# A decoder layer in split float32: other 16-byte places for the high weights of the up-projection and for the weights of the down-projection

## The chip, the cores and the metric

The kernel runs on one NeuronCore of a Trainium2 chip. The metric is device time in microseconds (us) of one execution. The kernel before takes 1066.99 us (median of 2 runs, 1066.96 to 1067.03).

## The reference

One layer for 256 tokens, model width 2048, all in float32. `w_in` feeds 16 heads of sliding-window attention with sinks and 16 heads of forgetting attention; the two groups are normalised, joined and go through `w_out`; then comes a gated MLP (5632 wide) with a causal convolution of width 3 between the up-projection and the activation. Every sub-layer is wrapped in two norms. What the change touches is the MLP:

```python
h = rmsnorm(x, pre_ffn_g[l])
u = causal_dwconv(h @ w_up[l], conv_w[l], conv_b[l])
gate, val = jnp.split(u, 2, axis=-1)
y = (jax.nn.gelu(gate, approximate=True) * val) @ w_down[l]
x = x + rmsnorm(y, post_ffn_g[l])
```

## The kernel before

**Split numbers.** [...] A product is then three matmuls: high by high, low by high, high by low. Weights come from HBM by SyncE's DMA queue into `raw` (512 KB, a ring of 5 buffers, line 71), ScalarE casts `raw` to the high part `whi` (line 117), VectorE subtracts to get the low part `wlo` (line 120). `whi` and `wlo` are rings of 5 buffers each. One such load is a *unit*.

**Up-projection: the weights are held.** `proj_T` (called 43 times for `w_up` with the order `LONG`, and with another order for `w_in`) makes 256 output columns. Its 16 k-tiles are four units of 4. In a matmul of a held weight, 128 columns of the weight are the stationary operand and `hT` (the activations, high and low side by side) is the moving operand: line 261 streams 512 columns of `hT` (high and low at once) past `whi`, line 268 streams 256 columns (high alone) past `wlo`. A unit gives 8 matmuls of each kind. `LONG = ((0, 1), (0, 1, 2, 3), (2, 3))` means: high of units 0 and 1, then low of units 0 to 3, then high of units 2 and 3. Since the next projection begins with its high units 0 and 1, TensorE sees runs of 32 high matmuls (512 columns) and runs of 32 low matmuls (256 columns) in turn. The first gate projection is written out by itself (lines 879 and 884), and its place in the program is not touched.

**Down-projection: the weights move.** For each half of the 5632 rows and each chunk of 512 output columns, 11 units of two k-tiles are loaded; `mm3` (line 283) holds 128 columns of the activations `G` and streams 512 columns of `whi`, `wlo`, `whi` past them: 12 matmuls a unit, 132 a chunk. Seven chunks go through the loop that the change touches (four of the first half, three of the second); the last chunk is written out apart.

**Places.** Buffers in SBUF lie on whole multiples of 256 bytes here. The kernel may start the data of a weight some 16-byte steps into its buffer. *Place* in this document means that number of steps (place 4 is 64 bytes in; place 16 is 256 bytes in). Before, all high parts and all moving weights are at place 0, as are `hT`, `G` and `oT`; the low parts of held weights are at `LOW = (14, 4, 4, 4)` for the units 0 to 3 of an up-projection, and at 14 and 4 in turn for `w_in` (function `w_parts`). The buffers of `whi` are 4096 bytes apart, those of `wlo` 4608.

**Order.** TensorE's instructions are kept in program order. The order on every other engine follows from the scheduler and, in some stretches, from manual order.

Of the kernel before, what the change touches and what calls it, by code (L numbers as in the profile page):

```python
# [8 lines left out]
F32 = mybir.dt.float32  # L9
F32R = mybir.dt.float32r  # L10
# [7 lines left out]
P = 128  # L18
# [7 lines left out]
FHALF = 22  # L26
HOLD = 6
LOW = (14, 4, 4, 4)
ROOM = 112


@with_exitstack
def hybrid_layer(ctx: ExitStack, tc: tile.TileContext, x, pre_mix_g, w_in, b_forget, sinks,
# [13 lines left out]

    small.tile([P, ROOM], F32, tag="room", bufs=1, name="room")
    ctx.enter_context(tc.manual_schedule(engines={mybir.EngineType.PE}))
# [7 lines left out]
    def tick():  # L57
        now[0] += 1
        for f in todo.pop(now[0], []):
            f()  # L60
# [5 lines left out]
    UNIT = 1024  # L66
    WB = 5

    def w_load(src, a, c, pin=False):
        raw = wp.tile([P, UNIT], F32, tag="raw", bufs=5, name="raw")  # L70
        i = sp.dma_start(raw[:, :a * c].rearrange("p (a c) -> p a c", a=a), src)
        if pin:
            tc.keep_in_program_order(i)
        return raw, a, c

    unit, period = [0], [2]

    def w_parts(n, keep=None, held=True):

        if keep and keep[0] is None:  # L80
            return keep[1]
        where, pre, nb = (keep[0], "h", keep[1]) if keep else (wp, "w", WB)
        hi = where.tile([P, UNIT], F32R, tag=pre + "hi", bufs=nb, name="whi")
        if where is not wp:
            lo = where.tile([P, UNIT], F32R, tag=pre + "lo", bufs=nb, name="wlo")
            return hi[:, :n], lo[:, :n]
        lo = where.tile([P, UNIT + 128], F32R, tag=pre + "lo", bufs=nb, name="wlo")
        at = 0
        if held:
            at = LOW[unit[0] % period[0]] * 4  # L90
            unit[0] += 1
        return hi[:, :n], lo[:, at:at + n]

    def w_high(unit, keep=None, held=True):

# [10 lines left out]
    def w_split(unit, pin=False, keep=None, begun=None, between=None,  # L106
                held=True):

        raw, a, c = unit
        n = a * c  # L110
        hi, lo = begun or w_parts(n, keep, held)
        for i in range(2 if between else 1):
            cs = slice(i * 512, i * 512 + 512) if between else slice(0, n)
            if i:
                between()
            if not between or i:
                i1 = act.copy(hi[:, cs], raw[:, cs])  # L117
                if pin:
                    tc.keep_in_program_order(i1)
            i2 = dve.tensor_tensor(lo[:, cs], raw[:, cs], hi[:, cs].bitcast(F32), op=ALU.subtract)  # L120
            if pin:
                tc.keep_in_program_order(i2)
        return [x.rearrange("p (a c) -> p a c", a=a) for x in (hi, lo)]

    def w_unit(src, a, c, keep=None):
        return w_split(w_load(src, a, c), keep=keep, held=False)

    def w_rows(w, k0, a, c0, c):
        return w[k0 * P:(k0 + a) * P, c0:c0 + c].rearrange("(a p) c -> p a c", p=P)
# [18 lines left out]
    for i in range(2):  # L148
        cs = slice(i * 256, (i + 1) * 256)
# [96 lines left out]
    def proj_T(w, c0, banks, runs=((0, 1), (0, 1), (2, 3), (2, 3))):  # L246

        parts, last = {}, ((len(runs) - 1) % 2, KT - 1)
        unit[0], period[0] = 0, 4 if len(runs) == 3 else 2

        def get(u):
            if u not in parts:
                parts[u] = w_split(w_load(w_rows(w, u * 4, 4, c0, 256), 4, 256))
            return parts[u]

        def high(u):
            hi = get(u)[0]
            for a in range(4):
                kt = u * 4 + a
                for m, b in enumerate(banks):  # L260
                    pe.matmul(b, hi[:, a, m * P:(m + 1) * P], hT[:, kt, 0:512], start=(kt == 0),  # L261
                              stop=(last == (0, kt)))

        def low(u):
            lo = get(u)[1]
            for a in range(4):
                for m, b in enumerate(banks):
                    pe.matmul(b[:, 256:512], lo[:, a, m * P:(m + 1) * P],  # L268
                              hT[:, u * 4 + a, 0:256], start=False,
                              stop=(last == (1, u * 4 + a)))  # L270

        for n, us in enumerate(runs):
            for u in us:
                (low if n % 2 else high)(u)
                tick()
# [13 lines left out]
    with tc.tile_pool(name="mixp", bufs=1) as mp:  # L289
# [311 lines left out]
        for p0, npair, cols in ((0, 3, 384), (3, 3, 384), (6, 2, 272)):  # L601
# [3 lines left out]
            for k0 in range(0, KT, per):  # L605
                na = min(per, KT - k0)
                hi, lo = w_unit(w_rows(w_in, k0, na, c0, cols), na, cols)
# [211 lines left out]
    with tc.tile_pool(name="ffn", bufs=1) as fp:  # L819
# [86 lines left out]
        for half in range(2):  # L906
            G = [fp.tile([P, 512], F32R, tag="G", bufs=FHALF, name=f"G{j}")[:, 0:512]
                 for j in range(FHALF)]
            for g in range(FHALF // 2):
                c0 = (half * (FHALF // 2) + g) * 256  # L910
                alt = g % 2
                if half == 0 and g == 0:
                    bg = first_gate()
                    order.__exit__(None, None, None)
                    bv = [bank(), bank()]
                    proj_T(w_up, DFF + c0, bv, LONG)
                else:
                    bg = [bank("att"), bank("att")] if alt else [bank(), bank()]
                    proj_T(w_up, c0, bg, LONG)
                gates = []  # L920
                for m in range(2):
                    y = conv(bg[m], c0 // P + m, "yg")
                    act.activation(y, y, AF.Gelu_apprx_tanh)
                    gates.append(y)
                if half or g:
                    bv = [bank("att"), bank("att")] if alt else [bank(), bank()]
                    proj_T(w_up, DFF + c0, bv, LONG)
                for m in range(2):
                    y = conv(bv[m], 44 + c0 // P + m, "yv")
                    dve.tensor_tensor(y, y, gates[m], op=ALU.mult)  # L930
                    gt = G[g * 2 + m]
                    split(gt[:, 0:256], gt[:, 256:512], y)
            if half == 1:
                rest = main.tile([P, KT, 512], F32R, tag="hT", name="rest")
                gbf = fp.tile([P, D], F32, tag="gbc", name="gbc_ffn")
                sp.dma_start(gbf, post_ffn_g[0].partition_broadcast(P))
                whole, halves = slice(0, 512), [slice(0, 256), slice(256, 512)]
                b1 = [bank("att"), bank("att")]
                for b, cs in zip(b1, halves):
                    pe.matmul(b[:, cs], G[0][:, 0:P], G[0][:, 0:256], start=True, stop=False)  # L940
                    act.copy(b[:, cs], y_sb[:, 1, 1536:2048][:, cs])

            def down(t, n, b):
                ys = y_sb[:, t, n * 512:(n + 1) * 512]
                if half == 0:
                    act.copy(ys, b)
                else:
                    dve.tensor_tensor(ys, b, ys, op=ALU.add)
                    act.activation(junk, ys, AF.Square, scale=D ** -0.5,
                                   accum_out=ysq[t][:, n:n + 1])  # L950
                    pool.tensor_tensor(ys, ys, gbf[:, n * 512:(n + 1) * 512], op=ALU.mult)

            LAST = FHALF // 2 - HOLD
            for n in range(3 + (half == 0)):
                b2 = [bank(), bank()]
                for u in range(FHALF // 2):
                    hi, lo = w_unit(w_rows(w_down, half * FHALF + u * 2, 2, n * 512, 512), 2, 512)
                    for a in range(2):
                        k = u * 2 + a
                        for t in range(2):  # L960
                            mm3(b2[t], G[k], t, hi[:, a, :], lo[:, a, :], slice(0, 512), k == 0,
                                k == FHALF - 1)
                for t in range(2):
                    down(t, n, b2[t])
# [32 lines left out]
        for u in range(FHALF // 2):  # L997
            hi, lo = w_unit(w_rows(w_down, FHALF + u * 2, 2, 1536, 512), 2, 512,
                            keep=(None, [rest[:, c:c + 2, :].rearrange("p a c -> p (a c)")
                                         for c in (4 * (u - LAST), 4 * (u - LAST) + 2)])  # L1000
                            if LAST <= u < FHALF // 2 - 4 else None)
# [13 lines left out]
        r = rstd_y(0, 3, v)  # L1015
        for n in range(4):
            finish(0, slice(n * 512, (n + 1) * 512), r, sp)
        last = fp.tile([P, 256], F32, tag="last", name="last")
        for h in range(2):
            if h:  # L1020
                v = before_last(1, 4)
# [38 lines left out]
```

## Time and profile before

| | |
|---|---|
| median of the runs | 1066.99 us |
| the profiled execution: its time, its span | 1067.17 us, 1065.3 us |
| TensorE matmul (PE) busy | 1055.4 us, 5974 instructions |
| weight loads (PEld) busy | 919.2 us, 5974 instructions |
| VectorE (DVE), ScalarE (ACT), GpSimd (POOL) busy | 738.3, 614.0, 226.2 us |
| mean granted TensorE clock | 0.998 |
| HBM read | 199.58 MB |

The span runs from the first to the last instruction; the 1.9 us between it and the execution's own time lie around it. Matmuls are pipelined, so the duration of one matmul (389 to 391 ns at 512 columns) is not what it costs. What it costs is the step from one matmul to the next, and that is read from the chain of waits: a piece there gives the start, the length and the number of matmuls, and the length divided by the number is the step. A row such as "7.29 PE bank_acc L261 x32" is a step of 228 ns.

### The profile page before, as it was taken

How to read it: one execution, taken by the hardware profiler on the slowest of the kernel's cores; microseconds unless marked ns; L12 is line 12 of the kernel's file. 1: busy time of each engine (PE TensorE's matmuls, PEld its weight loads, DVE VectorE, ACT ScalarE, POOL GpSimd, SP SyncE). 2: the span in 40 equal slices, each digit the busy share in tenths (PEclk: the TensorE clock that was granted, in tenths of full speed). 3: DMA queues.
4: the chain of work that ended last, by engine and by line, in shares of the span. 5: the costliest groups of instructions: out<-in, count | busy, mean ns of one | idle time of the engine just before them, and what ended most of it. 6: DMA issues, size and time to landing. Idle time of an engine off the chain costs nothing.

```text
span 1065.3 us, 16215 instructions
## 1 busy us (share of the span) xinstructions
PE 1055.4 (99%) x5974; PEld 919.2 (86%) x5974; DVE 738.3 (69%) x1200; ACT 614.0 (58%) x1062; POOL 226.2 (21%) x250
## 2 busy tenths in 40 slices
PE   9999999999999999999999999999999999999997
PEld 7889988888889888888888888888888888888886
DVE  5989868886568877777677444457777777755563
ACT  6776757767548655556565443456565555644450
POOL 4353245440122312112121000002121212201110
PEclk9999999999999999999999999999999999999999
DMA  8645667545863766566666666666666666666642
GB/s 290 191 127 175 181 191 213 176 153 160 296 223 122 236 197 193 183 198 197 197 187 185 202 196 195 194 186 198 183 199 192 195 181 198 197 195 194 192 170 79
DMA packets 164970, 202.88 MB, mean 190 GB/s; under 512 B 6780, under 2 KB 130972, under 8 KB 164380
## 3 DMA queue, kind: packets, MB, share of 16 engines
q1 hardware_dynamic: 164572, 201.45, 61.2%
q8 instruction: 47, 0.77, 0.3%
q10 hardware_dynamic: 320, 0.40, 0.1%
q14 instruction: 31, 0.25, 0.1%
HBM read 199.58 MB, written 2.11 MB: 189 GB/s over the span
## 4 chain that ended last, share of the span: by engine, by line
PE 94%; DVE 2%; issue 1%; DMA 1%; ACT 1%; POOL 1%; SPq 0%; DVEq 0%; POOLq 0%; ACTq 0%
PE bank_acc L283 34%; PE bank_acc L261 22%; PE bank_att L261 14%; PE bank_acc L268 11%; PE bank_att L268 7%; PE bank_att L449 1%; PE bank_att L484 1%; PE bank_att L493 1%; DVE wlo L120 1%; PE bank_acc L879 1%; PE bank_att L283 1%; DMA x_in<-in_x_dram 1%; PE bank_att L495 0%; PE bank_att L732 0%; POOL scr L416 0%
## 5 line engine op out<-in xcount | busy, mean ns | idle before, releaser
L120 DVE TENSOR_TENSOR wlo<-raw,whi 128x1024 fp32r<-128x1024 f32 (+3 forms) x357 | 435.7, 1230 | 239.1 <-ACT whi L117 232.7
L117 ACT CAST whi<-raw 128x1024 fp32r<-128x1024 f32 (+3 forms) x356 | 363.3, 1035 | 269.2 <-issue 121.2
L261 PE MATMUL bank_acc<-hT,whi 128*128 128x512 f32 x1088 | 260.6, 391 | 0.0
L261 PEld LDWEIGHTS bank_acc<-hT,whi 128*128 128x128 f32 x1088 | 200.1, 188 | 39.5
L283 PE MATMUL bank_acc<-whi,G 128*128 128x512 f32 x652 | 202.7, 389 | 0.0
L855 POOL TENSOR_TENSOR u<-u,rowf 128x256 f32<-128x256 f32 x88 | 96.6, 1118 | 493.5 <-DVE u L854 490.6
L261 PE MATMUL bank_att<-hT,whi 128*128 128x512 f32 x640 | 150.6, 390 | 0.0
L283 PEld LDWEIGHTS bank_acc<-whi,G 128*128 128x128 f32 x652 | 122.4, 188 | 25.0
L261 PEld LDWEIGHTS bank_att<-hT,whi 128*128 128x128 f32 x640 | 118.7, 188 | 23.9
L268 PEld LDWEIGHTS bank_acc<-hT,wlo 128*128 128x128 f32 x1088 | 131.1, 188 | 3.3
L268 PE MATMUL bank_acc<-hT,wlo 128*128 128x256 f32 x1088 | 133.4, 278 | 0.0
L283 PE MATMUL bank_acc<-wlo,G 128*128 128x512 f32 x326 | 126.9, 389 | 0.0
L283 PE MATMUL bank_acc<-whi,oT 128*128 128x512 f32 (+1 forms) x272 | 81.7, 379 | 0.0
L268 PEld LDWEIGHTS bank_att<-hT,wlo 128*128 128x128 f32 x640 | 76.0, 188 | 1.7
L268 PE MATMUL bank_att<-hT,wlo 128*128 128x256 f32 x640 | 76.3, 277 | 0.0
L283 PEld LDWEIGHTS bank_acc<-wlo,G 128*128 128x128 f32 x326 | 61.2, 188 | 12.3
L283 PEld LDWEIGHTS bank_acc<-whi,oT 128*128 128x128 f32 x272 | 50.2, 188 | 9.3
L283 PE MATMUL bank_acc<-wlo,oT 128*128 128x512 f32 (+1 forms) x136 | 51.2, 377 | 0.0
L283 PE MATMUL bank_acc<-whi,hT 128*128 128x384 f32 (+1 forms) x192 | 46.9, 323 | 0.0
L857 ACT ACTIVATE yg<-u,cw 128x256 f32<-128x256 f32 x44 | 26.5, 602 | 27.5 <-POOL u L855 27.5
L857 ACT ACTIVATE yv<-u,cw 128x256 f32<-128x256 f32 x44 | 26.4, 603 | 26.5 <-POOL u L855 26.5
L416 POOL TENSOR_TENSOR scr<-scr 128x256 f32<-128x256 f32 x26 | 26.7, 1042 | 57.2 <-DVE scr L415 34.3
(212 smaller groups left out, 1056.5 us busy)
## 6 DMA issues: line engine op xcount, KB each, us to landing
raw<-in_w_up_dram SPq DMA_DIRECT2D x176, 512.0 KB, 4.1
raw<-in_w_down_dram SPq DMA_DIRECT2D x88, 512.0 KB, 4.7
raw<-in_w_in_dram SPq DMA_DIRECT2D x51, 512.0 KB, 4.7
raw<-in_w_out_dram SPq DMA_DIRECT2D x32, 512.0 KB, 4.7
raw<-in_w_in_dram SPq DMA_DIRECT2D x16, 384.0 KB, 3.3
cb<-c_dram SPq DMA_DIRECT2D x8, 256.0 KB, 4.3
x_sb<-in_x_dram SPq DMA_DIRECT2D x2, 1024.0 KB, 5.9
raw<-in_w_in_dram SPq DMA_DIRECT2D x5, 408.0 KB, 4.1
```

Source lines behind the costliest of these rows:

```text
L117: i1 = act.copy(hi[:, cs], raw[:, cs])
L120: i2 = dve.tensor_tensor(lo[:, cs], raw[:, cs], hi[:, cs].bitcast(F32), op=ALU.subtract)
L261: pe.matmul(b, hi[:, a, m * P:(m + 1) * P], hT[:, kt, 0:512], start=(kt == 0), stop=(last == (0, kt)))
L268: pe.matmul(b[:, 256:512], lo[:, a, m * P:(m + 1) * P], hT[:, u * 4 + a, 0:256], start=False, stop=(last == (1, u * 4 + a)))
L283: pe.matmul(b, a, r[:, cols], start=(first and i == 0), stop=(last and i == 2))
L416: pool.tensor_tensor(dst, dst, row, op=ALU.mult)
L449: pe.matmul(sb[e][:, cs], a[r, t * P:(t + 1) * P], b[r, 0:nk], start=(n == 0), stop=(n == 2))
L484: pe.transpose(pb[:, i * P:(i + 1) * P], p[:, e, c:c + P], ident)
L493: pe.matmul(ov, values(hl, 0), p[:, :, 0:256], start=(n == 0), stop=False)
L855: pool.tensor_tensor(u[:, 2:258], u[:, 2:258], rowf, op=ALU.mult)
L857: act.activation(y, u[:, 2:258], AF.Identity, bias=cw[:, 3, ch:ch + 1], scale=cw[:, 2, ch:ch + 1])
L879: pe.matmul(v(b, t), gate[kt][0][:, ms], v(hT[:, kt, 0:512], t), start=(t == 0 and kt == 0), stop=False)
```

## The change

It changes where weights lie in their buffers, and nothing else: on each of the five engines the same instructions stand in the same order, with the same waits.

- The high parts of held weights in `w_up` get a place from the table `HIGH`. A row of it serves one run of 32 high matmuls: units 2 and 3 of a projection and units 0 and 1 of the next. There are 43 rows; of the last, only two entries are used. The first two units of all have place 0.
- The moving weights of `w_down` get places from the table `MOVE`: a row for each of the seven chunks, a pair (high part, low part) for each of the 11 units.
- The buffers of `whi` and `wlo` are all 4352 bytes apart now. The two rings take as many bytes together as before.
- The tile `last` of the final stretch takes a buffer of the ring `cs` in place of one of its own.
- The places of low parts of held weights stay as they were (`LOW`), and so do the high parts in `w_in` and `w_out`, and the last chunk of `w_down` (place 0).

```diff
 LOW = (14, 4, 4, 4)
+HIGH = (
+    (1,1,1,1), (2,2,2,2), (3,3,3,3), (4,4,4,4), (5,5,5,5), (6,6,6,6), (7,7,7,7),
+    (8,8,8,8), (9,9,9,9), (10,10,10,10), (11,11,11,11), (12,12,12,12), (13,13,13,13), (14,14,14,14),
+    (15,15,15,15), (2,4,4,4), (14,4,4,4), (12,4,4,4), (8,4,4,4), (10,4,4,4), (4,2,2,2),
+    (2,3,3,3), (0,4,4,4), (0,2,2,2), (0,1,1,1), (4,8,8,8), (8,12,12,12), (4,0,0,0),
+    (14,0,0,0), (2,0,0,0), (8,0,0,0), (12,0,0,0), (6,0,0,0), (0,2,4,6), (2,4,6,8),
+    (4,8,12,16), (1,2,3,4), (6,4,2,0), (0,4,0,4), (0,8,0,8), (0,16,0,16), (2,4,2,4),
+    (0,1,0,1),
+)
+MOVE = (
+    ((2, 2), (2, 2), (4, 4), (4, 4), (4, 4), (4, 4),
+     (12, 12), (12, 12), (4, 4), (4, 4), (4, 4)),
+    ((1, 1), (1, 1), (1, 1), (3, 3), (3, 3), (3, 3),
+     (5, 5), (5, 5), (5, 5), (6, 6), (6, 6)),
+    ((8, 8), (8, 8), (8, 8), (10, 10), (10, 10), (10, 10),
+     (14, 14), (14, 14), (14, 14), (16, 16), (16, 16)),
+    ((0, 4), (0, 4), (0, 4), (4, 0), (4, 0), (4, 0),
+     (0, 2), (0, 2), (0, 2), (0, 8), (0, 8)),
+    ((14, 14), (4, 4), (4, 4), (4, 4), (14, 14), (0, 0),
+     (0, 0), (0, 0), (2, 2), (0, 0), (0, 0)),
+    ((0, 0), (0, 0), (0, 0), (0, 0), (0, 0), (0, 0),
+     (12, 12), (12, 12), (12, 12), (15, 15), (15, 15)),
+    ((7, 7), (7, 7), (7, 7), (9, 9), (9, 9), (9, 9),
+     (11, 11), (11, 11), (11, 11), (13, 13), (13, 13)),
+)
...
-    unit, period = [0], [2]
+    unit, period, spot, turn_of = [0], [2], [(0, 0)], [-1]
...
-        hi = where.tile([P, UNIT], F32R, tag=pre + "hi", bufs=nb, name="whi")
         if where is not wp:
+            hi = where.tile([P, UNIT], F32R, tag=pre + "hi", bufs=nb, name="whi")
             lo = where.tile([P, UNIT], F32R, tag=pre + "lo", bufs=nb, name="wlo")
             return hi[:, :n], lo[:, :n]
-        lo = where.tile([P, UNIT + 128], F32R, tag=pre + "lo", bufs=nb, name="wlo")
-        at = 0
+        hi = where.tile([P, UNIT + 64], F32R, tag=pre + "hi", bufs=nb, name="whi")
+        lo = where.tile([P, UNIT + 64], F32R, tag=pre + "lo", bufs=nb, name="wlo")
+        (h, l), spot[0] = spot[0], (0, 0)
         if held:
-            at = LOW[unit[0] % period[0]] * 4
+            l = LOW[unit[0] % period[0]]
             unit[0] += 1
-        return hi[:, :n], lo[:, at:at + n]
+        return hi[:, h * 4:h * 4 + n], lo[:, l * 4:l * 4 + n]
...
         unit[0], period[0] = 0, 4 if len(runs) == 3 else 2
+        turn_of[0] += len(runs) == 3
 
         def get(u):
             if u not in parts:
+                j = turn_of[0] - (u < 2)
+                spot[0] = (HIGH[j][(u + 2) % 4] if j >= 0 else 0, 0)
                 parts[u] = w_split(w_load(w_rows(w, u * 4, 4, c0, 256), 4, 256))
             return parts[u]
...
                 for u in range(FHALF // 2):
+                    spot[0] = MOVE[half * 4 + n][u]
                     hi, lo = w_unit(w_rows(w_down, half * FHALF + u * 2, 2, n * 512, 512), 2, 512)
...
-        last = fp.tile([P, 256], F32, tag="last", name="last")
+        last = fp.tile([P, 256], F32, tag="cs", bufs=3, name="last")
```

## The prediction

> **What bounds the kernel now.** I read the page first, then TensorE's own waits, then the chain of waits stretch by stretch. The page:
>
> ```profile
> PE 1055.4 (99%) x5974; PEld 919.2 (86%) x5974; DVE 738.3 (69%) x1200; ACT 614.0 (58%) x1062; POOL 226.2 (21%) x250
> PEclk9999999999999999999999999999999999999999
> PE 94%; DVE 2%; issue 1%; DMA 1%; ACT 1%; POOL 1%; SPq 0%; DVEq 0%; POOLq 0%; ACTq 0%
> ```
>
> The waits of TensorE, all of them:
>
> ```profile
> PE bank_acc L172 <- DVE junk L167: 1.3, 1, 1.3
> PE bank_att L493 <- DVE pl L287: 0.4, 1, 0.4
> ```
>
> TensorE is busy 99% of the span at full granted clock, 94% of the chain is its own work, and it waits 1.7 us for others. So the time is the sum of its steps, and this change can act only on the step from one matmul to the next. The steps in the MLP, from the chain of waits (start, length, what; the steps are length by count):
>
> ```profile
> 386.47 7.29 PE bank_acc L261 x32
> 393.75 3.65 PE bank_acc L268 x32
> 576.10 119.68 PE bank_acc L283 x528
> 936.70 90.47 PE bank_acc L283 x399
> ```
>
> A held high matmul steps by 228 ns (7.29/32), a held low one, of half as many columns, by 114 ns, a matmul of `w_down` by 226.7 ns (119.68/528; 90.47/399 is the same). Inside a run the steps are not even. The first pieces of one run of highs and of one run of lows, and a piece farther on in each:
>
> ```profile
> 364.59 1.16 PE bank_att L261 x5
> 367.79 1.59 PE bank_att L261 x7
> 371.88 0.82 PE bank_att L268 x7
> 372.58 1.02 PE bank_att L268 x9
> ```
>
> The first five highs after the lows step by 232 ns, later ones by 227.1; the first seven lows (place 14) by 117.1, later ones (place 4) by 113.3. There is one more row, of `w_out`, with 256 moving columns and every operand at place 0 (lines 283, the two half chunks):
>
> ```profile
> 325.16 2.88 PE bank_acc L283 x24
> ```
>
> That is 120.0 ns for 256 columns. So for 256 columns the trace has three values: 120.0 at place 0, 117.1 in the unit at place 14, 113.3 at place 4, and no others. For 512 columns it has place 0 alone: 226.7 when it runs evenly, some 5 ns more for five matmuls after a switch. Whatever the mechanism is, place can matter by up to 6.7 ns a matmul (120.0 less 113.3), if it is the place that makes those rows differ: the lows also hold another tensor and read each moving tile twice.
>
> **The change part by part.**
>
> *Places of held highs.* 43 projections of 32 high matmuls are 1376. 137 of the entries used in `HIGH` are not multiples of 16, and each serves 8 matmuls: 1096 matmuls get another place, 272 of them place 4. *Places of moving weights.* 924 matmuls pass through `MOVE` (7 by 132), and 692 get another place (8 highs and 4 lows a unit), 156 of them place 4. Together 1788 matmuls, 428 at place 4, 1360 at others. The chain has no piece of 512 columns at such a place, so the cost is bounded by the rows above: 6.7 ns less a matmul at best, which would be 12.0 us over all 1788; at worst the step after a switch, 232 less 226.7, 5.3 ns more for good, or 9.5 us.
>
> - Place 4: I take the known 6.7 ns. 428 by 6.7 is 2.9 us less. Bounds: 0 (at 512 columns a weight load of the same size has twice the time) and 2.9.
> - Other places: the nearest row is place 14, 120.0 less 117.1, 2.9 ns, in a unit that also pays for a switch. I take half, 1.45 ns: 1360 by 1.45 is 2.0 us less. Bounds: 2.9 ns less (3.9 us) and 5.3 ns more.
> - Changes of place inside a run: 43 in `HIGH`; in `MOVE` 19, and 90 in the chunk where the high and low part lie at different places. Before, such a change is seen only in the lows (14 to 4), where the row of 113.3 ns shows no stall behind it; a change of width costs 5 by 5.3 ns, 26.5 ns. Between 0 and 26.5 I take 13 ns, as neither row is nearer: 152 by 13 is 2.0 us more.
>
> *The rings.* Buffers 4352 apart put every second buffer an odd multiple of 256 bytes from where it was. All buffers of before lie on multiples of 512, so no row shows what 256 bytes do. I take 0, since 64 bytes and 224 bytes give values within 6.7 ns; the bound is the rival below.
>
> *Casts and subtractions* write at other places, and their cover is large:
>
> ```profile
> L120 DVE TENSOR_TENSOR wlo<-raw,whi 128x1024 fp32r<-128x1024 f32 (+3 forms) x357 | 435.7, 1230 | 239.1 <-ACT whi L117 232.7
> L117 ACT CAST whi<-raw 128x1024 fp32r<-128x1024 f32 (+3 forms) x356 | 363.3, 1035 | 269.2 <-issue 121.2
> raw<-in_w_up_dram SPq DMA_DIRECT2D x176, 512.0 KB, 4.1
> ```
>
> VectorE stands idle 239 us before its 357 subtractions. A projection's four units take TensorE 10.94 us (7.29 and 3.65), and VectorE 4.9 us (four by 1230 ns) beside its convolution work; a tenth more on these would be 0.5 us a projection and stay hidden. Were the cover gone, the 36 us of a tenth would show. I count 0. DMAs move the same bytes, at the same points.
>
> *`last` in the ring `cs`.* Its buffer was read last when the up-projection ended, before 936.70; it is written behind the final matmuls. Cost 0; if it did wait it would be for work 100 us old.
>
> Sum: -2.9 - 2.0 + 2.0 is -2.9 us. The profiled execution of 1067.17 us would become 1064.3; against the median (1066.99, 0.18 lower) 1064.1 us.
>
> [...]
>
> **The rivals.**
>
> *No effect.* If the step of 226.7 ns at 512 columns is the streaming itself, and only the short matmuls of 256 columns, whose stationary load has half the time, feel a place, then the 1788 changed matmuls (all of 512 columns) step as before. For it: 512 columns run at 226.7 ns with `hT` and with `G` alike, and 226.7 is twice 113.3, the best row of 256. Against it: nothing in the trace. The time would be 1067.0. [...]
>
> *Restarts (slower).* Place 0 everywhere may be what lets the reads of weight and moving operand fall in step; each change of place puts them out of step as a change of width does, 26.5 ns a time. It decides if no place runs under 226.7 ns at 512 columns. 152 by 26.5 ns is 4.0 us: 1071.0. For it: the five steps of 232 ns behind each switch. Against it: the lows go from place 14 to 4 without any.
>
> *The rings (slower).* If two reads collide by their distance over 512 bytes rather than 256, half the low parts of held weights lie 256 bytes beside the good place. There are 1728 held lows (1088 and 640 in the rows below); with half of them back at 120.0 ns the cost is 864 by 6.7, 5.8 us, and the time 1072.8, or 1069.9 with the gains above.
>
> ```profile
> L268 PE MATMUL bank_acc<-hT,wlo 128*128 128x256 f32 x1088 | 133.4, 278 | 0.0
> L268 PE MATMUL bank_att<-hT,wlo 128*128 128x256 f32 x640 | 76.3, 277 | 0.0
> ```
>
> It decides if a low run has pieces of 120 ns in it that alternate with the buffer. Against it: nothing; for it: nothing but the common 512 of all old buffers.
>
> **How the numbers follow.** The forecast (a gain between 0.5 and 8 us) gets 0.45, no effect 0.25, restarts 0.2, the rings 0.1. The likeliest is 1064.1 us; its own range is 1059 to 1066.5. The range of 8 in 10 leaves out the forecast's far end (all places near the best, 1055.0, about one in ten) and the dearer half of the slower cases: 1059.0 to 1071.5. A change of 2% is 21.3 us, about what a measurement of this kernel can tell from no change. All 1788 at the best known value give 12.0 us, all at 5.3 ns more with the rings' 5.8 give 15.3, so neither side reaches it: within 2% 0.97, faster 0.015, slower 0.015, for what the rows of 256 columns don't bound.
>
> **What would show it.** In the chain after, each run of highs is a piece of 32. Under the forecast the runs of the rows with place 4 (the fourth row of `HIGH`, and the rows that end in three fours) shrink from 7.29 us towards 7.07, and the first chunk of `w_down` from 29.92 us (132 by 226.7 ns) by up to 0.9. Under no effect all stay at 7.29. Under restarts, runs of one place stay and runs of two to four places grow by 0.03 to 0.08 us, with the chunk of unequal pairs 2.4 us longer. Under the rings, runs of lows leave 3.65 us. The forecast is wrong if the run of place 4 isn't shorter than that of place 0 before, and my bounds are wrong if any run is over 7.46 us (32 steps of 233). TensorE's waits should stay under 2 us; if they grow, casts and subtractions were not covered.

## The result

The changed kernel takes 1077.97 us (median of 2 runs, 1077.93 to 1078.01) against 1066.99 before. The ratio is 1.0103, with a 95% interval from 1.0059 to 1.0146. It is slower by 11.0 us; the forecast was 2.9 us faster, and 1077.97 lies outside the range of 1059.0 to 1071.5. The profiled execution has a span of 1076.1 us, 10.8 more than before.

The page after, the lines that answer to those shown of before:

```profile
PE 1065.5 (99%) x5974; PEld 920.2 (86%) x5974; DVE 735.5 (68%) x1200; ACT 613.6 (57%) x1062; POOL 228.3 (21%) x250
PEclk9999999999999999999999999999999999999999
PE 96%; DVE 1%; issue 1%; DMA 1%; ACT 0%; SPq 0%; POOL 0%; DVEq 0%; POOLq 0%; ACTq 0%
```

TensorE is busy 10.1 us longer at the same granted clock (mean 0.998 in both) and with the same number of instructions; no other engine works more in any way that matters. The waits of TensorE, all of them:

```profile
PE bank_acc L198 <- DVE junk L193: 1.3, 1, 1.3
PE bank_att L522 <- DVE pl L316: 0.5, 1, 0.5
PE bank_acc L337 <- DMA x_in<-in_x_dram: 0.7, 1, 0.7
PE bank_att L337 <- DMA x_in<-in_x_dram: 0.2, 1, 0.2
```

They grew by 1.0 us, 0.9 of it in the first microseconds, where the first tile of x landed later; the matmuls of `junk` and the first transposes of x beside it take 0.9 us less (3.3 for 3.8 and 1.4 for 1.8), so that this cost nothing. None is behind a cast or a subtraction of weights: the wait for `pl`, a subtraction of the attention, was there before with 0.4. So the loss is in the steps. The groups of TensorE say which. First before (the groups of the held lows stand in the prediction), then after (line 290 is 261 of before, 297 is 268, 312 is 283):

```profile
L261 PE MATMUL bank_acc<-hT,whi 128*128 128x512 f32 x1088 | 260.6, 391 | 0.0
L283 PE MATMUL bank_acc<-whi,G 128*128 128x512 f32 x652 | 202.7, 389 | 0.0
L261 PE MATMUL bank_att<-hT,whi 128*128 128x512 f32 x640 | 150.6, 390 | 0.0
L283 PE MATMUL bank_acc<-wlo,G 128*128 128x512 f32 x326 | 126.9, 389 | 0.0
```

```profile
L290 PE MATMUL bank_acc<-hT,whi 128*128 128x512 f32 x1088 | 263.5, 394 | 0.0
L312 PE MATMUL bank_acc<-whi,G 128*128 128x512 f32 x652 | 205.7, 394 | 0.0
L290 PE MATMUL bank_att<-hT,whi 128*128 128x512 f32 x640 | 153.1, 394 | 0.0
L297 PE MATMUL bank_acc<-hT,wlo 128*128 128x256 f32 x1088 | 133.8, 278 | 0.0
L312 PE MATMUL bank_acc<-wlo,G 128*128 128x512 f32 x326 | 128.3, 394 | 0.0
L297 PE MATMUL bank_att<-hT,wlo 128*128 128x256 f32 x640 | 76.9, 278 | 0.0
```

The held highs take 5.4 us more (2.9 and 2.5), the moving weights of `w_down` 4.4 (3.0 and 1.4), and the held lows, whose own places did not change, 1.0 (0.4 and 0.6). That is 10.8, as much as the span grew.

The chain of waits gives it run by run. A run of 32 whose two halves write to the same group of accumulators (`bank_acc` or `bank_att`) is one piece of 32, the others are two of 16. In order of time, the rows of `HIGH` that these pieces belong to are (1,1,1,1) for the first two, then (2,2,2,2) with the lows behind it, (4,4,4,4), (6,6,6,6), (12,12,12,12), (15,15,15,15) as two pieces, (0,2,2,2), (0,1,1,1) as two pieces, (4,0,0,0) and (12,0,0,0):

```profile
353.55 3.73 PE bank_acc L290 x16
357.29 3.73 PE bank_att L290 x16
364.69 7.47 PE bank_att L290 x32
372.16 3.77 PE bank_att L297 x32
387.05 7.46 PE bank_acc L290 x32
409.28 7.50 PE bank_att L290 x32
476.21 7.33 PE bank_acc L290 x32
509.47 3.65 PE bank_att L290 x16
513.12 3.63 PE bank_acc L290 x16
731.83 7.44 PE bank_att L290 x32
742.93 3.65 PE bank_att L290 x16
746.59 3.63 PE bank_acc L290 x16
776.11 7.32 PE bank_att L290 x32
820.07 7.29 PE bank_att L290 x32
```

Before, every such run took 7.29 us (as two pieces 3.65 and 3.63, with the rounding). At places 1, 2, 4 and 6 it takes 7.46 to 7.50, a step of 233.1 to 234.4 ns. At place 15 it takes 7.28, no more than before, and at 12 it takes 7.33. No run is shorter than before: for 512 columns place 0 was already as good as the best place tried. Place 1 is the telling one. Alone it costs 0.17 us a run, in both halves alike (3.73 and 3.73), so the first unit alone does not pay it; behind one unit at place 0 it costs nothing. Place 2 is not like that: behind a unit at 0 the run still takes 7.44 us. And behind (2,2,2,2) the lows take 3.77 us instead of 3.65, although their own places did not change.

### The profile page after: what moved, and what is told of

Its sections match the earlier page's. It is cut to its first block, busy times and chain, and to the rows that moved or that the text cites. A ratio compares the mean times of both kernels' runs of the same rounds, so it can differ in the third digit from the quotient of the medians.

```text
span 1076.1 us, 16215 instructions
## 1 busy us (share of the span) xinstructions
PE 1065.5 (99%) x5974; PEld 920.2 (86%) x5974; DVE 735.5 (68%) x1200; ACT 613.6 (57%) x1062; POOL 228.3 (21%) x250
## 4 chain that ended last, share of the span: by engine, by line
PE 96%; DVE 1%; issue 1%; DMA 1%; ACT 0%; SPq 0%; POOL 0%; DVEq 0%; POOLq 0%; ACTq 0%
PE bank_acc L312 34%; PE bank_acc L290 23%; PE bank_att L290 14%; PE bank_acc L297 11%; PE bank_att L297 7%; PE bank_att L478 1%; PE bank_att L513 1%; PE bank_att L522 1%; PE bank_acc L908 1%; PE bank_acc L250 1%; PE bank_att L312 1%; DMA x_in<-in_x_dram 1%; PE bank_att L250 1%; PE bank_att L524 0%; PE bank_att L761 0%
## 5 line engine op out<-in xcount | busy, mean ns | idle before, releaser
L290 PE MATMUL bank_acc<-hT,whi 128*128 128x512 f32 x1088 | 263.5, 394 | 0.0
L312 PE MATMUL bank_acc<-whi,G 128*128 128x512 f32 x652 | 205.7, 394 | 0.0
L290 PE MATMUL bank_att<-hT,whi 128*128 128x512 f32 x640 | 153.1, 394 | 0.0
L297 PE MATMUL bank_acc<-hT,wlo 128*128 128x256 f32 x1088 | 133.8, 278 | 0.0
L297 PE MATMUL bank_att<-hT,wlo 128*128 128x256 f32 x640 | 76.9, 278 | 0.0
```

What stands on the lines that cost most here:

```text
L297: pe.matmul(b[:, 256:512], lo[:, a, m * P:(m + 1) * P], hT[:, u * 4 + a, 0:256], start=False, stop=(last == (1, u * 4 + a)))
L312: pe.matmul(b, a, r[:, cols], start=(first and i == 0), stop=(last and i == 2))
```

## The experiments

Two theories stood after that. **A: a carried state.** What matters is the distance, modulo 256 bytes, between the place of the moving operand and the place of the held weight, and the steps settle into one of a few even paces; which one depends on the distance and on the pace before. **B: the place of each matmul** has its price by itself. Beside them the rivals of the prediction: rings 256 bytes apart, restarts at each change.

**Only the rings.** `HIGH` and `MOVE` of the changed kernel at 0:

```diff
+HIGH = ((0, 0, 0, 0),) * 43
+MOVE = (((0, 0),) * 11,) * 7
```

> The changed kernel with every entry of HIGH and MOVE at 0: only the rings 256 bytes apart and the tile last in the ring cs stay. Theory A (the place inside 256 bytes decides, and multiples of 256 bytes do nothing): as before, 1067.0 us, runs of 32 highs at 7.29 us and of 32 lows at 3.65. Rival (the distance over 512 bytes decides): lows of every second buffer back at 120 ns, up to 5.8 us more, 1072.8.

Measured: 1067.21 us (before beside it 1067.2), ratio 0.9999, 0.999 to 1.0009. Runs of lows and highs in the chain:

```profile
448.56 3.65 PE bank_att L274 x32
452.21 7.29 PE bank_att L267 x32
```

The rings and the tile `last` cost nothing, and 256 bytes more or less between the operands are as good as none: the row (0,16,0,16) of the changed kernel takes 7.28 us too (3.65 and 3.63).

**The two parts apart.** Only `HIGH`, with `MOVE` at 0:

> The changed kernel with MOVE at 0: only the high parts of w_up have other places. Summed from the trace of the changed kernel (steps of its held highs: 5.4 us more than before; of its held lows, whose places did not change: 1.0 us more): 1073.4 us if the two parts of the change are independent. If the slower lows were due to something else than the highs before them, 1072.4.

Measured: 1073.55 us, ratio 1.006 (1.0045 to 1.0075). Only `MOVE`, with `HIGH` at 0:

> The changed kernel with HIGH at 0: only the moving weights of w_down have other places. Summed from the trace of the changed kernel (its seven chunks take 4.5 us more than before): 1071.5 us. If high places were the whole cause, 1067.0.

Measured: 1071.82 us, ratio 1.0043 (1.0028 to 1.0058). The parts are 6.35 and 4.6 us above the kernel before on their chip, 11.0 together: they add up to the whole. The slower lows come with the highs: the held lows take 1.0 us more than before in the first kernel (133.8 and 76.9 us busy) and nothing more in the second (133.4 and 76.3).

**Place or distance.** `hT` of the MLP and every held weight of `w_up` moved by 4 places (16 elements) together, with the rings 4352 bytes apart to make room:

```diff
-        hT2 = main.tile([P, KT, 512], F32R, tag="hT", name="hT2")
+        hT2 = main.tile([P, KT * 512 + 64], F32R, tag="hT", name="hT2")[:, 16:16 + KT * 512].rearrange("p (k c) -> p k c", k=KT)
...
-        return hi[:, :n], lo[:, at:at + n]
+        s = SHIFT[0] if held else 0
+        at = (at + s) % 64
+        return hi[:, s:s + n], lo[:, at:at + n]
...
         unit[0], period[0] = 0, 4
+        SHIFT[0] = 16
```

> The kernel before, with hT of the MLP and all held weights of w_up moved together by 4 places (64 bytes), high parts to 4 and low parts to 18 (2), 8, 8, 8. Theory A (only the distance between the moving operand and the weight being loaded matters, modulo 256 bytes): every step as before, 1067.0 us. Rival (the weight's own place in its 256 bytes matters, whatever the moving operand's): 43 runs of highs at place 4 take 174 ns more each as in the changed kernel, 7.5 us, 1074.5.

Measured: 1067.14 us, ratio 0.9999 (0.999 to 1.0009). Then `hT` alone (`s = 0` in the lines above), so that no weight moves:

> The kernel before, with hT of the MLP moved by 4 places and no weight moved. Theory A (the distance from the moving operand to the weight decides, modulo 16 places): highs are at distance 12, lows at 10, 0, 0, 0. A run of highs at place 12 took 41 ns more in the changed kernel; a run of lows with three units at place 0 took 159 to 190 ns more in the scan. By 43 runs 8.6 to 9.9 us: 1075.8 to 1077.1. Rival (the weight's own place, since no weight moves): 1067.2.

Measured: 1076.66 us, ratio 1.0089 (1.0073 to 1.0104). A run of lows and the highs behind it, of the kernel with `hT` alone moved:

```profile
449.78 3.83 PE bank_att L272 x32
453.62 7.33 PE bank_att L265 x32
```

With everything moved together nothing changes; with the activations moved under weights that stay, the highs take 7.33 us, as place 12 did in the changed kernel, and the lows 3.83. By 43 runs the highs make 1.7 us of it and the lows 7.7. The distance decides, not the weight's own place; nor is it a matter of the engines that write the weights, as casts and subtractions write to the same places in their buffers as in the kernel before. Where the activations lie against the weights is worth 9.3 us here (1076.66 for 1067.39 of the kernel before beside it).

**The carried state, highs.** All rows of `HIGH` at place 1, and all rows at (0, 1, 1, 1); `MOVE` at 0 in both:

```diff
+HIGH = ((1, 1, 1, 1),) * 43
```

> The changed kernel with MOVE at 0 and all 43 rows of HIGH at (1, 1, 1, 1). In the changed kernel the one such run took 7.460 us, 172 ns more than before, and the lows behind it 24 ns more. By 43 that is 8.4 us: 1075.4. Theory that the place of each matmul alone decides: 32 by 6.2 ns a run, the same 1075.

```diff
+HIGH = ((0, 1, 1, 1),) * 43
```

> As the run with place 1 throughout, but each row of HIGH is (0, 1, 1, 1): only the first unit behind the lows is at place 0. Theory A (a state that is carried from matmul to matmul: entered at place 0, the steps settle at 226.7 ns and place 1 keeps them there, as the one such run of the changed kernel did): 1067.0 us. Rival (the place of each matmul alone decides): three quarters of the loss with place 1 throughout, 1073.3.

Measured: 1075.22 us, ratio 1.0077 (1.0059 to 1.0095), and 1067.21 us, ratio 1.0 (0.999 to 1.0009). The same run in both kernels, place 1 throughout first:

```profile
453.67 7.46 PE bank_att L267 x32
```

```profile
451.73 7.29 PE bank_att L267 x32
```

24 of the 32 matmuls are at the same place in both kernels, and still the run takes 0.17 us more in one than in the other; by theory B three quarters of that loss would have stayed in the second. Theory B is out. So are the restarts: the kernel with a change of place in every run is the faster one.

**256 columns.** The low parts at place 0 in the up-projection:

```diff
-            at = LOW[unit[0] % period[0]] * 4
+            at = (0 if period[0] == 4 else LOW[unit[0] % period[0]]) * 4
```

> The kernel before, with the low parts of held weights of w_up at place 0 in place of (14, 4, 4, 4). If the row of 120.0 ns (256 columns, all at place 0) against 113.3 ns (lows at place 4) was a matter of place: 24 lows by 6.7 ns and 8 by 2.9 ns a run, 184 ns, by 44 runs 8.1 us more, 1075.1. If it was a matter of the tensor or of moving tiles read twice: 1067.0.

Measured: 1074.79 us, ratio 1.0072 (1.0054 to 1.009). A run of lows in it:

```profile
450.23 3.83 PE bank_att L268 x32
```

That is 119.7 ns a matmul: the row of 120.0 ns in the prediction was a matter of place, as I had supposed. Then a scan, with a table of places for the lows by projection:

> The kernel before, with another place of the low parts in each of the 43 projections: the same place 0 to 15 in all four units, then 14 in the first unit and 0 to 15 in the other three, then 0 to 10 in the first unit and 4 in the others. High parts at 0. [...]

The question is whether any place steps faster than the kernel before, whose runs of lows take 3.65 us; 32 steps of 120.0 ns are 3.84. Measured in one execution: 1071.56 us. Eight of its runs of lows, at (4,4,4,4), (8,8,8,8), (14,14,14,14), (14,4,4,4), (14,12,12,12), (0,4,4,4), (2,4,4,4) and (6,4,4,4):

```profile
394.19 3.77 PE bank_acc L280 x32
438.45 3.84 PE bank_acc L280 x32
504.93 3.73 PE bank_att L280 x32
571.25 3.65 PE bank_acc L280 x32
779.37 3.65 PE bank_att L280 x32
823.40 3.78 PE bank_att L280 x32
845.52 3.67 PE bank_acc L280 x32
889.64 3.67 PE bank_acc L280 x32
```

No run is below 3.65, so none of the places tried steps faster than the kernel before. All four units at place 14 take 3.73, which is 116.6 ns a matmul, and all four at place 4 take 3.77; with 14 in the first unit and 4 in the others they take 3.65, and 14 does the same for 12. It is not alone in this: with 2 or 6 in the first unit the run takes 3.67, with 7 to 10 it takes 3.68 to 3.70, while 0, 1, 3 and 5 leave it at 3.77 or 3.78. Place 4 throughout was tried on the whole kernel:

```diff
-            at = LOW[unit[0] % period[0]] * 4
+            at = (4 if period[0] == 4 else LOW[unit[0] % period[0]]) * 4
```

> The kernel before, with the low parts of w_up at place 4 in all four units, (4, 4, 4, 4) in place of (14, 4, 4, 4). Theory A (a carried state: the first unit behind the highs chooses it): the two such runs of the scan of low places took 3.77 us against 3.652 with 14 ahead, 117.5 ns more; by 43 runs 5.1 us, 1072.3 us. Rival (place 4 is the good place for 256 columns by itself): 1067.2 or, without the steps of place 14, 1.3 us less.

Measured: 1071.65 us, ratio 1.0039 (1.0025 to 1.0053). A run of lows in it and the highs behind:

```profile
449.11 3.77 PE bank_att L268 x32
452.88 7.28 PE bank_att L261 x32
```

That is 0.65 us under the expectation. The highs behind such lows are a little shorter (7.28 for 7.29 us, at the limit of the chain's rounding), which by 43 would be some 0.4 of it. That the pace hangs on the unit ahead is shown for the lows as well: 24 of the 32 are at place 4 in both kernels, in a run of 3.77 us behind a unit at place 4 and of 3.65 behind one at 14.

**A version that tries for a gain.** The rings of the changed kernel, `HIGH` and `MOVE` at 0, and the low parts' pattern for the high parts of the first gate projection, which streams 256 columns at place 0 in the kernel before:

```diff
+            spot[0] = (LOW[u], 0)
             (hi, lo), low = w_high(w_load(w_rows(w_up, u * 4, 4, 0, 256), 4, 256))
```

> The changed kernel with HIGH and MOVE at 0, and the high parts of the first gate projection (64 matmuls of 256 columns, at place 0, 120 ns each) at the places 14, 4, 4, 4 of the low parts. Theory A: most of these 64 go to 113.3 or 116.7 ns and the lows between them settle too, 0.3 to 0.45 us less: 1066.8. Rival (the transposes between the pieces reset the state): 0 to 0.1 us less. The difference may be too small for the interval of the times; the piece of 32 in the chain tells (3.84 us before; 3.65 by theory A).

Measured: 1066.99 us against 1067.39 beside it, ratio 0.9996 (0.9987 to 1.0005). The first 32 matmuls of that projection:

```profile
332.27 3.68 PE bank_acc L886 x32
```

The same 32 in the kernel before:

```profile
331.78 3.84 PE bank_acc L879 x32
```

The pieces behave as theory A says. The whole projection takes 0.2 us less in the chain (13.50 us, from 332.27 to 345.77, for 13.73, from 331.78 to 345.51), somewhat under what was expected; the 0.4 us between the medians is not resolved by the times.

## Why the prediction was wrong

- **What bounds the kernel: right.** The time is the sum of TensorE's steps, and the change acts on the step alone. Casts, subtractions, DMAs and `last` cost nothing.
- **Place 4: the step that failed.** I carried the 6.7 ns that place 4 saves at 256 columns over to 512 columns, and bounded it by 0 on the other side. At 512 columns a run at place 4 takes 7.46 us and not 7.07: 5.3 ns a matmul dearer than before. The place that is good for one width is bad for the other, and even at 256 columns it is good only behind some places (14, 2 and 6 to 10 in the scan, with 3.65 to 3.70 us a run, but not behind itself, with 3.77), which neither the row nor I could tell apart from the place itself. The trace before even had a second row of 256 columns at place 0, the 3.84 us of the first gate projection, with held weights; it would have made place the likelier reason at 256 columns, but it says nothing of 512.
- **Other places: wrong in sign.** I took half a gain of 2.9 ns. Of the runs of highs shown, only places 15 and 12 come near place 0, at 7.28 and 7.33 us. Over all 1788 changed matmuls the loss is 9.8 us (5.4 and 4.4), 5.5 ns each, where I had put 2.7 ns of gain (4.9 us). My dear end, 5.3 ns for good, which I had written down as a bound, was a little under the mean of what came; but I gave this case no rival and no chance of its own, and cut the range short of it.
- **A term I did not have:** the lows behind slower highs, 1.0 us, which hand over their pace.
- **Changes of place inside a run: no cost in themselves.** (0, 1, 1, 1) costs nothing in 43 runs. The row (4,0,0,0), with one change, takes 7.32 us, 0.03 more than before, against 0.17 for (4,4,4,4), with none.
- **The rings: 0, as taken.** Their rival is out by the run with both tables at 0.
- **The rivals.** No effect is out: the runs at places 1, 2, 4 and 6 say so. Restarts had the right side (slower) with the wrong mechanism: runs of one place throughout are among the dearest (7.46 to 7.50 us at places 1, 2, 4 and 6), and they were to stay at 7.29.
- **The signs I named** pointed the right way: the run of place 4 was not shorter, which I had called the end of the forecast, and the run at place 6 is over the 7.46 us beyond which my bounds were to be wrong.

The moving weights of `w_down` show a dependence on the units ahead too. Four windows of the chain after: in the first two all weights are at place 4, in the first behind units at place 2 and in the second behind one at 14; in the third they are at place 1, in the fourth at 15 behind 12:

```profile
586.85 9.15 PE bank_acc L312 x40
948.90 7.70 PE bank_acc L312 x33
612.85 5.33 PE bank_acc L312 x23
1000.81 5.20 PE bank_acc L312 x22
```

Place 4 steps by 228.8 ns in the one (9.15/40) and by 233.3 in the other (7.70/33). Places 1 and 15 step by 231.7 (5.33/23) and 236.4 (5.20/22), so there are more paces than the few of theory A; and 15, which cost nothing for the held highs, is here the dearest of the four. Before, all of this stepped by 226.7. No run moved `G` against these weights, so that the distance decides here as well is not shown.

## What to carry to other kernels

In this kernel, bound by back-to-back matmuls with a weight load each, the start addresses of the two operands modulo 256 bytes were a tuning knob: moving them cost up to 1% (1077.97 us for 1066.99), though nothing that was tried beat the kernel before by more than the times resolve. In another kernel bound in this way, try them per width of the moving operand, by the pace of whole runs and not by single matmuls. A good value found in one context did not carry to another width (place 4: 3.65 us a run at 256 columns behind 14, but 7.46 for 7.29 at 512) or to another predecessor (3.77 behind itself): try it in place, with the run ahead of it as it will be. When two bounds of an unknown cost lie on both sides of zero, the dear end is a rival and needs its own chance.

## What the runs showed of the hardware

- The step of a 512-column float32 matmul with its weight load was 226.7 ns with both operands at place 0 (`w_down` before). Held highs at other places took 7.28 us a run (place 15, and place 1 behind 0; 7.29 before), 7.33 (place 12), or 7.46 to 7.50 (places 1, 2, 4 and 6), which is 233.1 to 234.4 ns; moving weights stepped by 228.8 to 236.4 ns in the four windows. At 256 columns the runs of lows shown took 3.65 to 3.84 us, from 114 to 120 ns.
- In the up-projection the distance between moving operand and weight counted: both moved by 64 bytes, 1067.14 us; the moving operand alone, 1076.66. Rings of buffers 256 bytes off did nothing: 1067.21.
- The pace was carried: the same 24 matmuls at the same place sat in a run of 7.29 us or of 7.46, by the unit ahead of them. A whole run of lows was slower (3.77 for 3.65 us) because of the highs before it. Not every place kept the pace of the unit ahead: (0,2,2,2) took 7.44 us.
- Why the distance counts, and why the paces take these values, is not shown: no kernel without weight loads beside its matmuls was run.
